# The end of a diagonal-prefix-sum kernel reshaped: diagonal of the last rows first, last 128 rows folded on TensorE, last groups in halves

## The chip, the cores and the metric

The kernel runs on one core of a Trainium2 chip. The metric is device time in microseconds (us); a quoted time is the median of the runs of one kernel. The profile is one execution, and its span is some 2 us shorter than the time of the same run. Engines are named as in the profile: PE is TensorE, DVE is VectorE, ACT is ScalarE, POOL is GpSimd, SP is SyncE.

## The reference

```python
B, H, W = 4, 4224, 4224                      # x: (B, H, W) float32
ps   = np.cumsum(np.cumsum(x, axis=1), axis=2)
diag = np.diagonal(ps, axis1=1, axis2=2)     # (B, 4224)
return np.cumsum(diag, axis=1).astype(np.float32)
```

The element (i, i) of a 2-D prefix sum is the sum of the square up to row i and column i. Going from i-1 to i adds one row part (row i, columns up to i) and one column part (column i, rows above i). So each of the four matrices needs all its 71 MB once, and one number for each diagonal position comes out.

## The kernel before

A group is 384 rows, three to a partition; a matrix has 11 groups. One load brings a group into a strip and turns it into bf16 on the way. ACT and DVE sum the row parts. PE sums the columns with a selector of ones. For the square block on the diagonal, DVE multiplies with a triangular mask. The strip pool has six buffers. The loads are issued from POOL, in the order in which POOL's instructions stand. A scheduler in the build decides that order for the first three matrices.

```python
head = last.tile([P, HEAD], FP32, name="head")            # last 128 rows, last 1056 columns
nc.sync.dma_start(out=head, in_=x[LB, TB:N, N - HEAD : N])

def load_group(b, g):                                     # issued from POOL
    t = strips.tile([P, F, N], BF16, name="strip")
    ...
    nc.gpsimd.dma_start(out=t, in_=x[b, r0:r0+GW, :].rearrange("(p f) w -> p f w", f=F))
    return t

prefetched = {(0, g): load_group(0, g) for g in range(2)}
# ... masks and constants, among them
            um = consts.tile([P, P * f], BF16, name=f"um_{f}_{q}")
            nc.vector.memset(um, 1.0)
            nc.gpsimd.affine_select(out=um, in_=um, ..., pattern=[[1, P * f]], ...)
# ...
    nc.gpsimd.iota(apart_i, ...)                          # POOL
    nc.vector.tensor_copy(out=apart, in_=apart_i)         # DVE: int to float, "the cast"
    nc.gpsimd.affine_select(out=apart, in_=apart, ...)    # POOL: "the mask"; the load behind it waits too
```

The last matrix (b = 3) ends with 256 rows, two to a partition, and then 128 rows, one to a partition. Before, both are summed by ACT and DVE piece by piece as the loads land, and the final row of 128 results is built on one partition and stored:

```python
fin = psum_s.tile([1, P], FP32, name="fin")
matmul(fin, htot, wtri, start=True)
# for each loaded piece of the last 128 rows:
    nc.vector.reduce_sum(out=tsum[:, k:k+1], in_=tail[:, 0, c0:c1], axis=AX.X)
    matmul(fin, tsum[:, k:k+1], wtri)
yl = last.tile([1, P], FP32, name="yl")
nc.vector.tensor_add(out=yl, in0=fin, in1=lc[:, 1, gw:GW])
nc.sync.dma_start(out=out[b, TB:N].unsqueeze(0), in_=yl)
```

Of the kernel before, what the change touches and what calls it, by code (L numbers as in the profile page):

```python
# [8 lines left out]
FP32 = mybir.dt.float32  # L9
# [8 lines left out]
def kernel(  # L18
# [12 lines left out]
    N = H  # L31
# [20 lines left out]
    HEAD = 1056  # L52
    TB = N - P
    head = last.tile([P, HEAD], FP32, name="head")
    nc.sync.dma_start(out=head, in_=x[LB, TB:N, N - HEAD : N])

    def load_group(b, g):
        t = strips.tile([P, F, N], BF16, name="strip")
        r0 = g * GW
        nc.gpsimd.dma_start(  # L60
            out=t,
            in_=x[b, r0 : r0 + GW, :].rearrange("(p f) w -> p f w", f=F),
        )
        return t
# [12 lines left out]
    def upper_masks(f):  # L77
        ums = []
        for q in range(f):
            um = consts.tile([P, P * f], BF16, name=f"um_{f}_{q}")  # L80
# [7 lines left out]
                pattern=[[1, P * f]],  # L88
# [5 lines left out]
    um3 = upper_masks(F)  # L94
# [44 lines left out]
    um2 = upper_masks(2)  # L139
    um1 = upper_masks(1)[0]  # L140
# [13 lines left out]

    def matmul(o, lhsT, rhs, start=False):
        nc.tensor.matmul(  # L156
            o, lhsT=lhsT, rhs=rhs, start=start, stop=False, skip_group_check=True
        )

    DUMP = 2176  # L160

# [7 lines left out]
    def scalar_cols(g):  # L169
# [4 lines left out]
    hsum = last.tile([P, 2], FP32, name="hsum")  # L174
    hmu = last.tile([P, P], BF16, name="hmu")
    nc.vector.reduce_sum(out=hsum[:, 0:1], in_=head, axis=AX.X)
    nc.vector.scalar_tensor_tensor(
        out=hmu,
        in0=head[:, HEAD - P : HEAD],
        scalar=1.0,  # L180
        in1=um1,
        op0=ALU.mult,
        op1=ALU.mult,
        accum_out=hsum[:, 1:2],
    )
    htot = last.tile([P, 1], FP32, name="htot")
    nc.vector.tensor_sub(out=htot, in0=hsum[:, 0:1], in1=hsum[:, 1:2])
# [19 lines left out]
    for b in range(B):  # L207
        whole = b < LB
        ng = NG if whole else NG - 1
        d = psum_d.tile([NG, GW], FP32, name="d")  # L210
        d_last = None
        if not whole:
            d_last = psum_s.tile([1, GW], FP32, name="d_last")

        rs = smalls.tile([P, NG, F], FP32, name="rs")
        ru = smalls.tile([P, NG, F], FP32, name="ru")
        sa = smalls.tile([P, NG, F], FP32, name="sa")
        rows = smalls.tile([P, NG, F], FP32, name="rows")
        nc.vector.memset(sa[:, 0, :], 0.0)  # L219

        first = {"d": True, "l": True}

        def columns(j, lo, hi, rhs):

            if j < ng:
                matmul(d[:, lo:hi], selector(j), rhs, start=first["d"])
                first["d"] = False
            else:
                matmul(d_last[:, lo:hi], ones_col, rhs, start=first["l"])
                first["l"] = False  # L230

        for g in range(ng):
            lo, hi = g * GW, (g + 1) * GW
            strip = prefetched.pop((b, g), None)
            if strip is None:
                strip = load_group(b, g)
            ws = scalar_cols(g)
            for q in range(F):
                mu = mup.tile([P, GW], BF16, name="mu")
                nc.vector.scalar_tensor_tensor(  # L240
                    out=mu,
                    in0=strip[:, q, lo:hi],
                    scalar=1.0,
                    in1=um3[q],
                    op0=ALU.mult,
                    op1=ALU.mult,
                    accum_out=ru[:, g, q : q + 1],
                )
# [36 lines left out]
        if whole:  # L285
            continue
# [113 lines left out]
```

## Time and profile before

| | before |
|---|---|
| time, first three runs | 675.43 us (674.44 to 675.74) |
| span of the profiled run | 672.8 us |
| DVE, PE busy | 39%, 35% of the span |
| written by the loads | 217 GB/s in nearly every slice |
| last load lands (its issue plus "us to landing") | 634.5 + 28.8 = 663.3 us |
| last store issued, and the span's end after it | 670.82 us, 1.98 us |

The page of the kernel before. The rows DMA and GB/s have one figure for each of 40 equal slices of the span; a 9 is 90% or more.

```profile
span 672.8 us, 2608 instructions
...
DMA  9999999999999999999999999999999999999994
GB/s 202 217 215 218 217 217 217 217 217 217 217 219 217 217 218 217 217 217 217 217 217 218 218 217 217 217 215 217 218 217 217 217 217 218 217 217 217 217 201 76
```

The load queue never runs dry until the last slice. So the time is the bytes, plus what comes before the first byte and after the last one.

The start in the timeline of POOL (start, duration, line and instruction, and in brackets what ended the idle time):

```profile
1.32 1.19 POOL L60 DMA_DIRECT2D strip<-in_x_dram  x2 [0.80 <-POOLq L384]
...
6.01 0.58 POOL L60 DMA_DIRECT2D strip<-in_x_dram  x1
38.57 0.19 POOL L130 TENSOR_SCALAR_AFFINE_SELECT apart<-apart 11x11 f32<-11x11 f32 x1 [31.98 <-DVE apart L129]
...
39.49 1.61 POOL L60 DMA_DIRECT2D strip<-in_x_dram  x3
```

Two strips are asked for at 1.32 us, a third at 6.01 (strips are counted from 0, so the third load brings strip 2). Then POOL stands for 32 us in front of the mask of `apart`, which waits for DVE's cast. Nobody is hurt, because the third load is already in the queue.

The last load of the kernel before, in the timeline of POOL and then in its DMA issues (KB, us from issue to landing):

```profile
634.53 0.53 POOL L308 DMA_DIRECT2D strip<-in_x_dram  x1 [14.41 <-DMA strip<-in_x_dram]
```

```profile
strip<-in_x_dram POOLq DMA_DIRECT2D x1, 132.0 KB, 28.8
```

The end in the timeline, the last DVE steps and the last store (SPq):

```profile
665.40 0.96 DVE L362 TENSOR_REDUCE tsum<-strip 128x1 f32<-128x792 bf16 x1
...
666.36 1.23 DVE L362 TENSOR_REDUCE tsum<-strip 128x1 f32<-128x1056 bf16 x1
...
667.89 1.00 DVE L190 TENSOR_TENSOR_SCAN lc<-ones_row,lcarry,d_last 1x384 f32<-1x384 f32 x1 [0.30 <-PE d_last L156]
668.82 0.67 DVE L362 TENSOR_REDUCE tsum<-strip 128x1 f32<-128x528 bf16 x1
669.42 0.99 DVE L198 TENSOR_TENSOR_SCAN lc<-ones_row,lcarry,lc 1x384 f32<-1x384 f32 x1
...
670.51 0.28 DVE L368 TENSOR_TENSOR yl<-fin,lc 1x128 f32<-1x128 f32 x1
670.82 0.23 SPq L369 DMA_DIRECT2D out_dram<-yl  x1
```

About 7.5 us of serial work (663.3 to 670.8) stand between the last landing and the last store, which itself takes 2.0 us to the end.

### The profile page before, as it was taken

What the parts mean: (1) busy time and instruction counts of PE and PEld (TensorE: products, weight loads), DVE (VectorE), ACT (ScalarE), POOL (GpSimd) and SP (SyncE); (2) the same over time, 40 slices, a digit from 0 to 9 for tenths busy, and PEclk for the clock granted to TensorE, in tenths of its full rate; (3) what the DMA queues carried; (4) which work ended last, traced back from release to release, by engine and by line L of the source; (5) the groups of instructions that cost most, each with busy time, mean ns of one, the idle gap of its engine ahead of it and who ended that gap; (6) DMA issues with size and microseconds to landing.
All of it is one profiled execution on the core that took longest, in us unless ns stands there. A gap on an engine that the chain in (4) does not pass through costs nothing.

```text
span 672.8 us, 2608 instructions
## 1 busy us (share of the span) xinstructions
PE 232.5 (35%) x852; PEld 91.2 (14%) x852; DVE 259.3 (39%) x370; ACT 153.9 (23%) x249; POOL 31.8 (5%) x67
## 2 busy tenths in 40 slices
PE   0073453211155543321116543232204534344213
PEld 0031111000022211100002211110001211111001
DVE  2033333344543223334563222334555222234458
ACT  0011222233301112223420111223440011123342
POOL 3010000000000000000000000000000000100000
PEclk9997766555577766566557766766555776766655
DMA  9999999999999999999999999999999999999994
GB/s 202 217 215 218 217 217 217 217 217 217 217 219 217 217 218 217 217 217 217 217 217 218 218 217 217 217 215 217 218 217 217 217 217 218 217 217 217 217 201 76
DMA packets 7958, 143.23 MB, mean 213 GB/s; under 512 B 861, under 2 KB 1546, under 8 KB 2442
## 3 DMA queue, kind: packets, MB, share of 16 engines
q0 software_dynamic: 7712, 142.47, 99.0%
q1 hardware_dynamic: 234, 0.61, 0.3%
q8 instruction: 6, 0.10, 0.1%
q14 instruction: 6, 0.05, 0.0%
HBM read 285.47 MB, written 0.07 MB: 424 GB/s over the span
## 4 chain that ended last, share of the span: by engine, by line
another core or an unknown queue 51%; DVE 36%; DMA 11%; issue 1%; POOL 0%; PE 0%; DVEq 0%; POOLq 0%
DVE rs L252 24%; DMA strip<-in_x_dram 11%; DVE mu L240 9%; DVE lrs L334 1%; DVE c L198 1%; DVE c L190 1%; DVE y L281 0%; DVE y L273 0%; DVE tsum L362 0%; POOL strip L60 0%; DVE lc L190 0%; DVE lc L198 0%; PE d_last L156 0%; DVEq L240 0%
## 5 line engine op out<-in xcount | busy, mean ns | idle before, releaser
L165 ACT ACTIVATE dump<-strip 128x192 bf16<-128x192 bf16 (+11 forms) x124 | 141.1, 1138 | 507.7 <-DMA strip<-in_x_dram 505.1
L240 DVE SCALAR_TENSOR_TENSOR mu<-strip,um 128x384 bf16<-128x384 bf16 x129 | 65.5, 554 | 380.9 <-DMA strip<-in_x_dram 380.9
L252 DVE TENSOR_REDUCE rs<-strip 128x3 f32<-128x1152 bf16 (+10 forms) x43 | 169.8, 3950 | 27.5 <-DMA strip<-in_x_dram 27.5
L156 PE MATMUL d<-mu,sel 128*11 128x384 bf16 x129 | 59.2, 476 | 318.8 <-DVE mu L240 318.5
L156 PE MATMUL d<-strip,sel 128*11 128x384 bf16 x630 | 161.9, 431 | 0.0
L156 PEld LDWEIGHTS <-sel 128*11 128x11 bf16 (+1 forms) x794 | 86.7, 109 | 538.8 <-issue 515.2
L60 POOL DMA_DIRECT2D strip<-in_x_dram x43 | 23.0, 535 | 507.5 <-PE d L156 256.7
L156 PE MATMUL d_last<-strip,sel 128*1 128x384 bf16 (+1 forms) x32 | 14.2, 477 | 84.8 <-DMA strip<-in_x_dram 84.8
L165 ACT ACTIVATION_READ_ACCUMULATOR dump<-strip 128x1 f32 x124 | 23.1, 186 | 0.0
L156 PE MATMUL d<-ident,rows 128*11 128x128 f32 (+1 forms) x24 | 5.8, 415 | 19.9 <-DVE sa L219 13.2
L240 DVE DVE_READ_ACCUMULATOR mu<-strip,um 128x1 f32 x129 | 10.5, 82 | 0.0
L156 PEld LDWEIGHTS d<-ident,rows 128*11 128x11 f32 (+1 forms) x24 | 2.7, 128 | 24.0 <-DVE sa L219 15.0
L156 PE MATMUL fin<-wtri,tsum 128*1 128x128 f32 x8 | 2.4, 401 | 6.7 <-DVE tsum L362 3.9
L334 DVE TENSOR_REDUCE lrs<-strip 128x2 f32<-128x1664 bf16 (+2 forms) x3 | 4.4, 1459 | 0.0
L198 DVE TENSOR_TENSOR_SCAN c<-ones_row,c 11x384 f32<-11x384 f32 (+1 forms) x4 | 3.8, 940 | 0.0
L190 DVE TENSOR_TENSOR_SCAN c<-ones_row,d 11x384 f32<-11x384 f32 (+1 forms) x4 | 3.7, 935 | 0.0
L308 POOL DMA_DIRECT2D strip<-in_x_dram x3 | 1.6, 538 | 43.1 <-DMA strip<-in_x_dram 28.5
L362 DVE TENSOR_REDUCE tsum<-strip 128x1 f32<-128x792 bf16 (+2 forms) x3 | 2.9, 952 | 0.0
L156 PE MATMUL d_last<-mu,sel 128*1 128x256 bf16 x2 | 0.8, 396 | 5.5 <-DVE mu L316 5.5
L304 POOL DMA_DIRECT2D strip<-in_x_dram x3 | 2.1, 708 | 6.7 <-DMA strip<-in_x_dram 6.7
L82 POOL TENSOR_SCALAR_AFFINE_SELECT um<-um 128x384 bf16<-128x384 bf16 (+2 forms) x6 | 2.4, 434 | 0.1
L281 DVE TENSOR_TENSOR y<-y,c 11x384 f32<-11x384 f32 (+1 forms) x4 | 2.2, 545 | 0.1
(56 smaller groups left out, 24.1 us busy)
## 6 DMA issues: line engine op xcount, KB each, us to landing
strip<-in_x_dram POOLq DMA_DIRECT2D x43, 3168.0 KB, 81.7
strip<-in_x_dram POOLq DMA_DIRECT2D x1, 832.0 KB, 72.7
strip<-in_x_dram POOLq DMA_DIRECT2D x1, 672.0 KB, 75.2
head<-in_x_dram SPq DMA_DIRECT2D x1, 528.0 KB, 3.8
strip<-in_x_dram POOLq DMA_DIRECT2D x1, 416.0 KB, 69.8
strip<-in_x_dram POOLq DMA_DIRECT2D x1, 396.0 KB, 56.5
strip<-in_x_dram POOLq DMA_DIRECT2D x1, 264.0 KB, 43.1
strip<-in_x_dram POOLq DMA_DIRECT2D x1, 192.0 KB, 69.4
```

What stands on the lines that cost most here:

```text
L60: nc.gpsimd.dma_start(out=t, in_=x[b, r0 : r0 + GW, :].rearrange("(p f) w -> p f w", f=F),)
L82: nc.gpsimd.affine_select(out=um, in_=um, compare_op=ALU.is_gt, fill=0.0, base=-q, pattern=[[1, P * f]], channel_multiplier=-f,)
L156: nc.tensor.matmul(o, lhsT=lhsT, rhs=rhs, start=start, stop=False, skip_group_check=True)
L165: nc.scalar.activation(out=dump[:, :w], in_=src, func=ACT.Copy, accum_out=acc)
L190: nc.vector.tensor_tensor_scan(out=c12[:rows, 0, :width], data0=ones_row[:rows, :width], data1=d, initial=init1, op0=ALU.mult, op1=ALU.add,)
L198: nc.vector.tensor_tensor_scan(out=c12[:rows, 1, :width], data0=ones_row[:rows, :width], data1=c12[:rows, 0, :width], initial=init2, op0=A ...
L240: nc.vector.scalar_tensor_tensor(out=mu, in0=strip[:, q, lo:hi], scalar=1.0, in1=um3[q], op0=ALU.mult, op1=ALU.mult, accum_out=ru[:, g, q ...
L252: nc.vector.reduce_sum(out=rs[:, g, :], in_=strip[:, :, ws:hi], axis=AX.X)
L281: nc.vector.tensor_add(out=y[:ng, :], in0=y[:ng, :], in1=c12[:ng, 1, :])
L304: nc.gpsimd.dma_start(out=strip[:, :2, c0:c1], in_=src[:, :, c0:c1])
L334: nc.vector.reduce_sum(out=lrs[:, :, i + 1], in_=strip[:, :2, c0 + ws : c1], axis=AX.X)
L362: nc.vector.reduce_sum(out=tsum[:, k : k + 1], in_=tail[:, 0, c0:c1], axis=AX.X)
```

## The change

The intent is to shorten those 7.5 us. The diagonal blocks of the last 384 rows are loaded at the very start, so that these rows end as plain row sums. The last 128 rows are weighted and summed on PE, which folds their 3968 columns into 256, and DVE sums these. The last two full groups are loaded in halves, so that about half of their row sums is done before the group is complete. In each group PE's column matmuls stand ahead of the diagonal products. The last matrix is built in program order and not by the scheduler. Cut to its core:

```diff
-    head = last.tile([P, HEAD], FP32, name="head")
-    nc.sync.dma_start(out=head, in_=x[LB, TB:N, N - HEAD : N])
+    head_a = last.tile([P, 2, GW], FP32, name="head_a")
+    nc.sync.dma_start(out=head_a, in_=x[LB, T0:TB, T0:N].rearrange("(p f) w -> p f w", f=2))
+    head_b = last.tile([P, HB], FP32, name="head_b")
+    nc.sync.dma_start(out=head_b, in_=x[LB, TB:N, N - HB : N])
...
-    def load_group(b, g):
+    def load_group(b, g, cut=0):
+        if cut:
+            nc.gpsimd.dma_start(out=t[:, :, :cut], in_=src[:, :, :cut])
+            nc.gpsimd.dma_start(out=t[:, :, cut:], in_=src[:, :, cut:])
...
-            um = consts.tile([P, P * f], BF16, name=f"um_{f}_{q}")
+            um = consts.tile([P, w], BF16, name=f"um_{f}_{q}")
...
-                pattern=[[1, P * f]],
+                pattern=[[1, w]],
...
-    um2 = upper_masks(2)
+    um2 = upper_masks(2, GW)                 # 256 columns become 384
...
+        if not whole:
+            ctx.enter_context(tc.manual_schedule())
...
-        tcuts = [N - HEAD, 1584, 528, 0]
+        tcuts = [(2176, N - HB), (640, 2176), (128, 640), (0, 128)]
...
-        fin = psum_s.tile([1, P], FP32, name="fin")       # sums by DVE, row on one partition
-        ...
-        nc.sync.dma_start(out=out[b, TB:N].unsqueeze(0), in_=yl)
+        fold = psum_s.tile([P, 2 * P], FP32, name="fold")
+        matmul(fold[:, 0:1], wtri, hrow[:, 2:3], start=True)
+        for c0, c1 in tcuts:
+            if c0 == 0:
+                matmul(fold[:, 0:1], lc[:, 1, 2 * P : GW], ones_row[:1, :1])
+            while c0 < c1:
+                w = min(2 * P, c1 - c0)
+                matmul(fold[:, :w], wtri_h, tail[:, 0, c0 : c0 + w])
+                c0 += w
+        yl = last.tile([P, 1], FP32, name="yl")
+        nc.vector.reduce_sum(out=yl, in_=fold, axis=AX.X)
+        nc.sync.dma_start(out=out[b, TB:N].unsqueeze(1), in_=yl)   # one number from each partition
```

What the build makes of POOL's order, before and after (cut from the listings of the built programs, not a profile). Only the place of one load changes:

```
before: ... iota apart_i, 3 selects of um, iota wtri_i, LOAD strip 2, mask apart, mask wtri, LOAD strips 3, 4, 5
after:  ... iota apart_i, 3 selects of um, iota wtri_i, mask apart, LOAD strip 2, mask wtri, LOAD strips 3, 4, 5
```

More of the change, by code (lines that the diff above doesn't have):

```diff
@@ L49 @@
     )
-    HEAD = 1056
     TB = N - P
-    head = last.tile([P, HEAD], FP32, name="head")
-    nc.sync.dma_start(out=head, in_=x[LB, TB:N, N - HEAD : N])
-    def load_group(b, g):
+    T0 = N - GW
+    HB = 2 * P
+    head_a = last.tile([P, 2, GW], FP32, name="head_a")
+    nc.sync.dma_start(
+        out=head_a, in_=x[LB, T0:TB, T0:N].rearrange("(p f) w -> p f w", f=2)
+    )
+    head_b = last.tile([P, HB], FP32, name="head_b")
+    nc.sync.dma_start(out=head_b, in_=x[LB, TB:N, N - HB : N])
+    def load_group(b, g, cut=0):
         t = strips.tile([P, F, N], BF16, name="strip")
         r0 = g * GW
-        nc.gpsimd.dma_start(
-            out=t,
-            in_=x[b, r0 : r0 + GW, :].rearrange("(p f) w -> p f w", f=F),
-        )
+        src = x[b, r0 : r0 + GW, :].rearrange("(p f) w -> p f w", f=F)
+        if cut:
+            nc.gpsimd.dma_start(out=t[:, :, :cut], in_=src[:, :, :cut])
+            nc.gpsimd.dma_start(out=t[:, :, cut:], in_=src[:, :, cut:])
+        else:
+            nc.gpsimd.dma_start(out=t, in_=src)
         return t
@@ L75, in selector, with upper_masks @@
         return sel[:, NG - 1 - j : 2 * NG - 1 - j]
-    def upper_masks(f):
+    def upper_masks(f, w):
         ums = []
         for q in range(f):
-            um = consts.tile([P, P * f], BF16, name=f"um_{f}_{q}")
+            um = consts.tile([P, w], BF16, name=f"um_{f}_{q}")
             nc.vector.memset(um, 1.0)
@@ L92, in upper_masks @@
         return ums
-    um3 = upper_masks(F)
+    um3 = upper_masks(F, GW)
     ident = consts.tile([P, P], FP32, name="ident")
@@ L138 @@
     )
-    um2 = upper_masks(2)
-    um1 = upper_masks(1)[0]
+    um2 = upper_masks(2, GW)
+    um1 = upper_masks(1, P)[0]
     wtri_i = consts.tile([P, P], I32, name="wtri_i")
@@ L153 @@
     )
+    wtri_h = consts.tile([P, P], BF16, name="wtri_h")
+    nc.vector.tensor_copy(out=wtri_h, in_=wtri)
     def matmul(o, lhsT, rhs, start=False):
@@ L160 @@
     DUMP = 2176
+    CUT = 2176
     def act_sum(acc, src):
@@ L171, in scalar_cols @@
         return 0 if g == 0 else (g * GW) * 9 // 16 // 32 * 32
-    hsum = last.tile([P, 2], FP32, name="hsum")
-    hmu = last.tile([P, P], BF16, name="hmu")
-    nc.vector.reduce_sum(out=hsum[:, 0:1], in_=head, axis=AX.X)
-    nc.vector.scalar_tensor_tensor(
-        out=hmu,
-        in0=head[:, HEAD - P : HEAD],
-        scalar=1.0,
-        in1=um1,
-        op0=ALU.mult,
-        op1=ALU.mult,
-        accum_out=hsum[:, 1:2],
-    )
-    htot = last.tile([P, 1], FP32, name="htot")
-    nc.vector.tensor_sub(out=htot, in0=hsum[:, 0:1], in1=hsum[:, 1:2])
+    hs = last.tile([P, 3], FP32, name="hs")
+    hu = last.tile([P, 3], FP32, name="hu")
+    hrow = last.tile([P, 3], FP32, name="hrow")
+    hmu_a = last.tile([P, 2, GW], BF16, name="hmu_a")
+    hmu_b = last.tile([P, P], BF16, name="hmu_b")
+    nc.vector.reduce_sum(out=hs[:, 0:2], in_=head_a, axis=AX.X)
+    nc.vector.reduce_sum(out=hs[:, 2:3], in_=head_b, axis=AX.X)
+    for k, o, i, m in (
+        (0, hmu_a[:, 0, :], head_a[:, 0, :], um2[0]),
+        (1, hmu_a[:, 1, :], head_a[:, 1, :], um2[1]),
+        (2, hmu_b, head_b[:, HB - P : HB], um1),
+    ):
+        nc.vector.scalar_tensor_tensor(
+            out=o,
+            in0=i,
+            scalar=1.0,
+            in1=m,
+            op0=ALU.mult,
+            op1=ALU.mult,
+            accum_out=hu[:, k : k + 1],
+        )
+    nc.vector.tensor_sub(out=hrow, in0=hs, in1=hu)
     def scans(d, rows, width, init1, init2, c12):
@@ L205, in scans @@
         )
-    for b in range(B):
-        whole = b < LB
-        ng = NG if whole else NG - 1
-        d = psum_d.tile([NG, GW], FP32, name="d")
-        d_last = None
-        if not whole:
-            d_last = psum_s.tile([1, GW], FP32, name="d_last")
-        rs = smalls.tile([P, NG, F], FP32, name="rs")
-        ru = smalls.tile([P, NG, F], FP32, name="ru")
-        sa = smalls.tile([P, NG, F], FP32, name="sa")
-        rows = smalls.tile([P, NG, F], FP32, name="rows")
-        nc.vector.memset(sa[:, 0, :], 0.0)
-        first = {"d": True, "l": True}
-        def columns(j, lo, hi, rhs):
-            if j < ng:
-                matmul(d[:, lo:hi], selector(j), rhs, start=first["d"])
-                first["d"] = False
-            else:
-                matmul(d_last[:, lo:hi], ones_col, rhs, start=first["l"])
-                first["l"] = False
-        for g in range(ng):
-            lo, hi = g * GW, (g + 1) * GW
-            strip = prefetched.pop((b, g), None)
-            if strip is None:
-                strip = load_group(b, g)
-            ws = scalar_cols(g)
-            for q in range(F):
-                mu = mup.tile([P, GW], BF16, name="mu")
-                nc.vector.scalar_tensor_tensor(
-                    out=mu,
-                    in0=strip[:, q, lo:hi],
-                    scalar=1.0,
-                    in1=um3[q],
-                    op0=ALU.mult,
-                    op1=ALU.mult,
-                    accum_out=ru[:, g, q : q + 1],
-                )
-                columns(g, 0, GW, mu)
-                if ws > 0:
-                    act_sum(sa[:, g, q : q + 1], strip[:, q, :ws])
-            nc.vector.reduce_sum(
-                out=rs[:, g, :], in_=strip[:, :, ws:hi], axis=AX.X
-            )
-            for j in range(g + 1, NG):
-                for q in range(F):
-                    columns(j, 0, GW, strip[:, q, j * GW : (j + 1) * GW])
-        nc.vector.tensor_add(out=rows[:, :ng], in0=rs[:, :ng], in1=sa[:, :ng])
-        nc.vector.tensor_sub(out=rows[:, :ng], in0=rows[:, :ng], in1=ru[:, :ng])
-        for q in range(F):
-            matmul(d[:ng, q : GW : F], rows[:, :ng, q], ident)
-        c12 = smalls.tile([NG, 2, GW], FP32, name="c12")
-        scans(d[:ng, :], ng, GW, 0.0, 0.0, c12)
-        carry_ps = psum_s.tile([NG, 2], FP32, name="carry_ps")
-        matmul(carry_ps[:ng, :], earlier[:ng, :ng], c12[:ng, :, GW - 1], start=True)
-        matmul(carry_ps[:ng, 1:2], apart[:ng, :ng], c12[:ng, 0, GW - 1 : GW])
@@ L270, with between @@
+    def between(b, ng, c12, carry_ps):
         carry = smalls.tile([NG, 2], FP32, name="carry")
@@ L284, with columns @@
         )
+    for b in range(B):
+        whole = b < LB
+        if not whole:
+            ctx.enter_context(tc.manual_schedule())
+        ng = NG if whole else NG - 1
+        d = psum_d.tile([NG, GW], FP32, name="d")
+        d_last = None
+        if not whole:
+            d_last = psum_s.tile([1, GW], FP32, name="d_last")
+        first = {"d": True, "l": True}
+        def columns(j, lo, hi, rhs):
+            if j < ng:
+                matmul(d[:, lo:hi], selector(j), rhs, start=first["d"])
+                first["d"] = False
+            else:
+                matmul(d_last[:, lo:hi], ones_col, rhs, start=first["l"])
+                first["l"] = False
+        rs = smalls.tile([P, NG, F], FP32, name="rs")
+        ru = smalls.tile([P, NG, F], FP32, name="ru")
+        sa = smalls.tile([P, NG, F], FP32, name="sa")
+        rows = smalls.tile([P, NG, F], FP32, name="rows")
+        nc.vector.memset(sa[:, 0, :], 0.0)
+        if not whole:
+            rs2 = last.tile([P, 2, F], FP32, name="rs2")
+            sa2 = last.tile([P, 2, F], FP32, name="sa2")
+            for q in range(2):
+                columns(NG - 1, 0, GW, hmu_a[:, q, :])
+            columns(NG - 1, GW - P, GW, hmu_b)
+            for q in range(2):
+                matmul(d_last[:, q : 2 * P : 2], hrow[:, q : q + 1], ident)
+        for g in range(ng):
+            lo, hi = g * GW, (g + 1) * GW
+            strip = prefetched.pop((b, g), None)
+            cut = 0
+            if strip is None:
+                cut = CUT if not whole and g >= ng - 2 else 0
+                strip = load_group(b, g, cut)
+            ws = scalar_cols(g)
+            if cut:
+                ws1 = cut * 5 // 8 // 32 * 32
+                for q in range(F):
+                    act_sum(sa2[:, g - ng + 2, q : q + 1], strip[:, q, :ws1])
+                nc.vector.reduce_sum(
+                    out=rs2[:, g - ng + 2, :], in_=strip[:, :, ws1:cut], axis=AX.X
+                )
+                ws = cut + (lo - cut) * 5 // 8 // 32 * 32
+            for j in range(g + 1, NG):
+                for q in range(F):
+                    columns(j, 0, GW, strip[:, q, j * GW : (j + 1) * GW])
+            for q in range(F):
+                mu = mup.tile([P, GW], BF16, name="mu")
+                nc.vector.scalar_tensor_tensor(
+                    out=mu,
+                    in0=strip[:, q, lo:hi],
+                    scalar=1.0,
+                    in1=um3[q],
+                    op0=ALU.mult,
+                    op1=ALU.mult,
+                    accum_out=ru[:, g, q : q + 1],
+                )
+                columns(g, 0, GW, mu)
+                if ws > 0:
+                    act_sum(sa[:, g, q : q + 1], strip[:, q, cut:ws])
+            nc.vector.reduce_sum(
+                out=rs[:, g, :], in_=strip[:, :, ws:hi], axis=AX.X
+            )
+        if not whole:
+            nc.vector.tensor_add(out=rs2, in0=rs2, in1=sa2)
+            nc.vector.tensor_add(
+                out=rs[:, ng - 2 : ng], in0=rs[:, ng - 2 : ng], in1=rs2
+            )
+        nc.vector.tensor_add(out=rows[:, :ng], in0=rs[:, :ng], in1=sa[:, :ng])
+        nc.vector.tensor_sub(out=rows[:, :ng], in0=rows[:, :ng], in1=ru[:, :ng])
+        for q in range(F):
+            matmul(d[:ng, q : GW : F], rows[:, :ng, q], ident)
+        c12 = smalls.tile([NG, 2, GW], FP32, name="c12")
+        scans(d[:ng, :], ng, GW, 0.0, 0.0, c12)
+        carry_ps = psum_s.tile([NG, 2], FP32, name="carry_ps")
+        matmul(carry_ps[:ng, :], earlier[:ng, :ng], c12[:ng, :, GW - 1], start=True)
+        matmul(carry_ps[:ng, 1:2], apart[:ng, :ng], c12[:ng, 0, GW - 1 : GW])
@@ L285 @@
         if whole:
+            between(b, ng, c12, carry_ps)
             continue
@@ L293 @@
         nc.vector.tensor_copy(out=lcarry, in_=lcarry_ps)
-        columns(NG - 1, 2 * P, GW, hmu)
-        r0 = ng * GW
-        gw = 2 * P
+        src = x[b, T0:TB, :].rearrange("(p f) w -> p f w", f=2)
         strip = strips.tile([P, F, N], BF16, name="strip")
-        src = x[b, r0 : r0 + gw, :].rearrange("(p f) w -> p f w", f=2)
-        cuts = [r0, 2176, 832, 0]
-        nc.gpsimd.dma_start(out=strip[:, :2, r0:N], in_=src[:, :, r0:N])
-        for c1, c0 in zip(cuts[:-1], cuts[1:]):
+        cuts = [(1920, T0), (640, 1920), (0, 640)]
@@ L304 @@
+        for c0, c1 in cuts:
             nc.gpsimd.dma_start(out=strip[:, :2, c0:c1], in_=src[:, :, c0:c1])
         tail = strips.tile([P, F, N], BF16, name="strip")
-        tcuts = [N - HEAD, 1584, 528, 0]
-        for c1, c0 in zip(tcuts[:-1], tcuts[1:]):
+        tcuts = [(2176, N - HB), (640, 2176), (128, 640), (0, 128)]
+        for c0, c1 in tcuts:
             nc.gpsimd.dma_start(out=tail[:, 0, c0:c1], in_=x[b, TB:N, c0:c1])
-        NP = len(cuts)
-        lrs = last.tile([P, 2, NP], FP32, name="lrs")
@@ L312 @@
-        lru = last.tile([P, 2], FP32, name="lru")
-        lsa = last.tile([P, 2, NP - 1], FP32, name="lsa")
-        for q in range(2):
-            mu = mup.tile([P, GW], BF16, name="mu")
-            nc.vector.scalar_tensor_tensor(
-                out=mu[:, :gw],
-                in0=strip[:, q, r0 : r0 + gw],
-                scalar=1.0,
-                in1=um2[q],
-                op0=ALU.mult,
-                op1=ALU.mult,
-                accum_out=lru[:, q : q + 1],
-            )
-            columns(NG - 1, 0, gw, mu[:, :gw])
-            columns(NG - 1, gw, GW, strip[:, q, r0 + gw : N])
@@ L327 @@
-        nc.vector.reduce_sum(
-            out=lrs[:, :, 0], in_=strip[:, :2, r0 : r0 + gw], axis=AX.X
-        )
-        for i, (c1, c0) in enumerate(zip(cuts[:-1], cuts[1:])):
-            ws = (c1 - c0) // 2
-            for q in range(2):
-                act_sum(lsa[:, q, i : i + 1], strip[:, q, c0 : c0 + ws])
-            nc.vector.reduce_sum(
-                out=lrs[:, :, i + 1], in_=strip[:, :2, c0 + ws : c1], axis=AX.X
-            )
-        l1 = last.tile([P, 2], FP32, name="l1")
-        l2 = last.tile([P, 2], FP32, name="l2")
@@ L339, with to_row @@
-        lrows = last.tile([P, 2], FP32, name="lrows")
-        nc.vector.reduce_sum(out=l2, in_=lsa, axis=AX.X)
-        nc.vector.tensor_sub(out=l2, in0=l2, in1=lru)
-        nc.vector.reduce_sum(out=l1, in_=lrs, axis=AX.X)
-        nc.vector.tensor_add(out=lrows, in0=l1, in1=l2)
-        for q in range(2):
-            matmul(d_last[:, q : gw : 2], lrows[:, q : q + 1], ident)
+        def to_row(a):
+            for q in range(2):
+                matmul(d_last[:, q : 2 * P : 2], a[:, q : q + 1], ident)
@@ L346 @@
+        lsa = last.tile([P, 3, 2], FP32, name="lsa")
+        for i, (c0, c1) in enumerate(cuts):
+            act_sum(lsa[:, i, 0:1], strip[:, 0, c0:c1])
+            if i == 0:
+                act_sum(lsa[:, i, 1:2], strip[:, 1, c0:c1])
+            else:
+                nc.vector.reduce_sum(
+                    out=lsa[:, i, 1:2], in_=strip[:, 1, c0:c1], axis=AX.X
+                )
+            to_row(lsa[:, i, :])
         lc = last.tile([1, 2, GW], FP32, name="lc")
         scans(d_last, 1, GW, lcarry[:, 0:1], lcarry[:, 1:2], lc)
-        nc.sync.dma_start(out=out[b, r0 : r0 + gw].unsqueeze(0), in_=lc[:, 1, :gw])
@@ L351 @@
-        fin = psum_s.tile([1, P], FP32, name="fin")
-        matmul(fin, htot, wtri, start=True)
-        tsum = last.tile([P, 4], FP32, name="tsum")
-        k = 0
-        for i, (c1, c0) in enumerate(zip(tcuts[:-1], tcuts[1:])):
-            if i == 0:
-                ws = (c1 - c0) // 2
-                act_sum(tsum[:, k : k + 1], tail[:, 0, c0 : c0 + ws])
-                matmul(fin, tsum[:, k : k + 1], wtri)
-                k += 1
-                c0 += ws
-            nc.vector.reduce_sum(
-                out=tsum[:, k : k + 1], in_=tail[:, 0, c0:c1], axis=AX.X
-            )
-            matmul(fin, tsum[:, k : k + 1], wtri)
-            k += 1
@@ L367 @@
-        yl = last.tile([1, P], FP32, name="yl")
-        nc.vector.tensor_add(out=yl, in0=fin, in1=lc[:, 1, gw:GW])
-        nc.sync.dma_start(out=out[b, TB:N].unsqueeze(0), in_=yl)
+        between(b, ng, c12, carry_ps)
+        nc.sync.dma_start(out=out[b, T0:TB].unsqueeze(0), in_=lc[:, 1, : 2 * P])
+        fold = psum_s.tile([P, 2 * P], FP32, name="fold")
+        matmul(fold[:, 0:1], wtri, hrow[:, 2:3], start=True)
+        for c0, c1 in tcuts:
+            if c0 == 0:
[4 more added lines that the diff above has]
+                c0 += w
```

## The prediction

> **What bounds it now.** The loads. In the page's 40 slices the DMA share is nine tenths or more in every slice but the last, at 217 GB/s written (424 GB/s read; the Trainium skill, "DMA: Bandwidth & Descriptors", "Where 436 GB/s comes from", gives about 358 per core from HBM, so the trace decides). DVE is busy 39%, PE 35%: shorter compute in the middle buys nothing. Only two places pay: a hole in the load stream, and what follows the last byte. By short windows the stream ends at 662.4 us; the last load lands about 663.4 (issue at 634.5 plus 28.8); the span is 672.8. So 9.4 us follow the last landing: in the timeline DVE scans, carries, three tail sums (0.96, 1.23, 0.67 us), two one-partition scans (1.0 each), an add, then the store (2.0 us from issue to end).
>
> **Intended gain: the tail.** Bytes are equal. My estimate of the new tail from those durations: last group lands 649.8, its shorter reduction (2592 elements at 1.04 ns, against 6.15 us before) ends 654.2, group scans 658.2, the two remaining row reductions 661.4, the one-row scans 664.0, carry and y 665.0. PE folds 3968 columns of the last 128 rows in 17 matmuls; at the granted clock of 0.5 a 384-column one repeats every 0.32 us, so 0.21 to 0.32 us each; the last 128 columns land near 664.2 and the fold ends near 666. One PSUM reduction (0.4 us), then the store of 128 four-byte pieces (2.0 to 2.4 us). End near 669: gain 3.7 us (2.5 to 5), after some 0.8 us lost to smaller packets.
>
> **Cost that the diff does not show: the third strip load.** The instruction order of the built kernels differs on POOL. Before, the third strip load is issued (6.01 us) ahead of the masking of "apart"; after, behind it. That mask waits for DVE's cast of "apart", which stands behind DVE's row sums of strips 0 and 1 and three masked products; in the timeline the cast ran at 38.34 and the mask at 38.57 to 38.76. Strip 1's data ends about 33.7 (landing 34.77). So the queue would hold nothing from about 33.3 (mean over engines) until the load issued at 38.8 delivers, about 1.5 us after issue (first load: issue 1.3, data 2.85), near 40.3. A hole of some 7 us, and since the stream is saturated after it, all of it reaches the end.
>
> **Sum.** 675.4 + 7.0 - 3.7 = 678.7 us; range 675.8 to 681.5. Faster by over 2%: 1%; within 2%: 97%; slower by over 2%: 2%.
>
> **What would show it.** DMA share near zero in windows from about 34 to 40 us; the third strip landing near 56 instead of 49.8; every later group some 7 us later; in the chain of waits the DVE and POOL steps of "apart". After the last landing: 4 to 6 us instead of 9.4, ending in fold on PE, one reduction of yl, one store. The middle keeps 217 GB/s and 15 us per group.
>
> **What would make it wrong.** The third load is not blocked (then about 671.7). The fold at low clock is slower than 0.32 us each, or the scattered four-byte store takes over 3 us: then the tail gains less. The skill's same page ("Specifications") says that pieces under 512 B are read and rewritten; the trace shows 79 ns for a 768-byte packet against 1887 ns for 25 KB, and no smaller load packet. Engine skew of 1 to 2 us at the ends of loads blurs the hole.

## The result

The changed kernel takes 684.3 us (683.34 to 684.54, 4 runs), the kernel before in the same job 674.98 us (4 runs). The ratio is 1.0135 (95% interval 1.0117 to 1.0152). Ratios here are the mean time of one kernel's fast runs over that of the other's of the same rounds, so not quite the ratio of the medians. The change is slower by 1.4%, and 684.3 is above the stated range.

The page of the changed kernel, the same rows:

```profile
span 681.5 us, 2655 instructions
...
DMA  8969999999999999999999999999999999999993
GB/s 199 213 123 223 223 216 214 214 216 215 214 219 220 221 220 214 214 214 218 216 217 221 218 219 214 214 217 219 216 216 221 218 217 214 214 219 208 215 212 73
```

The third slice (34 to 51 us) falls to 123 GB/s. Later slices have the old rate. POOL and DVE at the start of the changed kernel:

```profile
1.31 1.19 POOL L71 DMA_DIRECT2D strip<-in_x_dram  x2 [0.80 <-POOLq L401]
...
38.73 1.06 POOL L138 TENSOR_SCALAR_AFFINE_SELECT apart<-apart 11x11 f32<-11x11 f32 x1 [32.46 <-DVE apart L137]
39.75 0.58 POOL L71 DMA_DIRECT2D strip<-in_x_dram  x1
```

```profile
34.93 1.95 DVE L313 TENSOR_REDUCE rs<-strip 128x3 f32<-128x1728 bf16 x1 [13.08 <-DMA strip<-in_x_dram]
...
38.50 0.15 DVE L137 CAST apart<-apart_i 11x11 f32<-11x11 int32 x1
```

DVE's cast of `apart` (38.50) stands behind the row sum of strip 1, which could only start when that strip landed (34.93), and behind three masked products cut from the view. The mask follows the cast at 38.73, and the third load follows the mask at 39.75. The windows view of the changed kernel shows what the load engines did meanwhile (last two columns: DMA share, GB/s):

```profile
33.00:37.00 4.00, 0.00 (x0) 0.00 (x0) 2.07 (x2) 1.37 (x6) 0.00 (x0) 0.50 0.01 0
37.00:41.00 4.00, 3.59 (x11) 1.32 (x11) 4.00 (x21) 0.00 (x0) 2.26 (x3) 0.50 0.00 0
41.00:45.00 4.00, 4.00 (x25) 2.09 (x24) 0.77 (x5) 0.00 (x0) 2.77 (x5) 0.96 1.11 203
```

The start of strip 2's work on ACT marks its landing. These are one line of the kernel before and one of the changed kernel:

```profile
49.79 0.55 ACT L165 ACTIVATE dump<-strip 128x416 bf16<-128x416 bf16 x1 [13.59 <-DMA strip<-in_x_dram]
```

```profile
57.58 0.55 ACT L177 ACTIVATE dump<-strip 128x416 bf16<-128x416 bf16 x1 [21.23 <-DMA strip<-in_x_dram]
```

So it landed 7.8 us later (57.58 against 49.79). The last load of the changed kernel, in the timeline of POOL and in the DMA issues:

```profile
650.42 0.53 POOL L352 DMA_DIRECT2D strip<-in_x_dram  x1 [7.24 <-DMA strip<-in_x_dram]
```

```profile
strip<-in_x_dram POOLq DMA_DIRECT2D x1, 32.0 KB, 21.2
```

The end of the changed kernel, the last DVE step and the stores (`y` holds the results of the ten full groups, `lc` those of the 256 rows, `yl` the last 128), and the last store's line in the DMA issues:

```profile
672.92 0.28 SPq L240 DMA_DIRECT2D out_dram<-y  x1
...
673.25 0.25 SPq L372 DMA_DIRECT2D out_dram<-lc  x1
...
673.70 0.42 DVE L385 TENSOR_REDUCE yl<-fold 128x1 f32<-128x256 f32 x1 [0.80 <-PE fold L167]
674.15 0.36 SPq L386 DMA_DIRECT2D out_dram<-yl  x1
```

```profile
out_dram<-yl SPq DMA_DIRECT2D x1, 0.5 KB, 6.5
```

The last store is issued at 674.15 and the span ends at 681.5, 7.35 us later. Before it was 1.98 us for the same 512 bytes. The DMA engines are not at work in most of that time, as two lines of the windows view of the changed kernel show (last two columns again DMA share, GB/s):

```profile
675.00:676.00 1.00, 0.00 (x0) 0.00 (x0) 0.00 (x0) 0.00 (x0) 0.00 (x0) 1.00 0.08 1
676.00:677.00 1.00, 0.00 (x0) 0.00 (x0) 0.00 (x0) 0.00 (x0) 0.00 (x0) 0.62 0.00 0
```

The same zero stands in every window after that. So the pieces are on record as moved before 676, but the landing is signalled only at 674.15 + 6.5 = 680.7. What holds the landing back is not in the trace.

All of the difference of the two spans, 681.5 - 672.8 = 8.7 us, can be added up from three places:

| place | before | after | difference |
|---|---|---|---|
| last load lands (issue + landing) | 663.3 | 650.4 + 21.2 = 671.6 | +8.3 |
| from there to the issue of the last store | 7.5 | 2.5 | -5.0 |
| from that issue to the span's end | 1.98 | 7.35 | +5.4 |

Of the first row, 7.8 us are there when strip 2 lands; the other 0.5 us come by the end. Smaller pieces are the likely cause; no run isolates it.

### The profile page after: what moved, and what is told of

It reads as the page before. It is cut to its first block, busy times and chain, and to the rows that moved or that the text cites. A ratio compares the mean times of both kernels' runs of the same rounds, so it can differ in the third digit from the quotient of the medians.

```text
span 681.5 us, 2655 instructions
## 1 busy us (share of the span) xinstructions
PE 230.0 (34%) x872; PEld 97.6 (14%) x872; DVE 254.6 (37%) x367; ACT 156.7 (23%) x255; POOL 35.4 (5%) x69
## 4 chain that ended last, share of the span: by engine, by line
another core or an unknown queue 50%; DVE 34%; DMA 12%; PE 2%; issue 1%; DVEq 0%; POOL 0%; POOLq 0%
DVE rs L313 23%; DMA strip<-in_x_dram 12%; DVE mu L301 9%; PE d L167 1%; DVE rs L292 1%; PE fold L167 1%; DVE c L218 1%; DVE c L210 1%; DVE y L239 0%; PE d_last L167 0%; DVE lsa L364 0%; DVE y L231 0%; DVE rows L322 0%; DVE rows L323 0%
## 5 line engine op out<-in xcount | busy, mean ns | idle before, releaser
L167 PE MATMUL d<-strip,sel 128*11 128x384 bf16 x630 | 177.5, 462 | 353.8 <-DMA strip<-in_x_dram 353.8
L177 ACT ACTIVATE dump<-strip 128x640 bf16<-128x640 bf16 (+12 forms) x127 | 143.6, 1131 | 510.7 <-DMA strip<-in_x_dram 508.1
L313 DVE TENSOR_REDUCE rs<-strip 128x3 f32<-128x2208 bf16 (+11 forms) x43 | 163.5, 3801 | 13.1 <-DMA strip<-in_x_dram 13.1
L167 PEld LDWEIGHTS <-sel 128*11 128x11 bf16 (+1 forms) x792 | 90.0, 114 | 539.0 <-issue 506.6
L167 PE MATMUL d<-mu,sel 128*11 128x384 bf16 x129 | 38.4, 403 | 50.9 <-DVE mu L301 50.9
L167 PE MATMUL d_last<-strip,sel 128*1 128x384 bf16 x30 | 8.7, 410 | 12.1 <-DMA strip<-in_x_dram 12.1
L292 DVE TENSOR_REDUCE rs<-strip 128x3 f32<-128x2496 bf16 x2 | 5.5, 2754 | 5.0 <-DMA strip<-in_x_dram 5.0
L167 PE MATMUL fold<-strip,wtri_h 128*128 128x256 bf16 (+1 forms) x16 | 3.4, 387 | 0.0
L167 PE MATMUL d_last<-ident,lsa 128*1 128x128 f32 x12 | 2.9, 406 | 0.2 <-DVE lsa L364 0.2
```

The costliest lines, as they stand in the source:

```text
L167: nc.tensor.matmul(o, lhsT=lhsT, rhs=rhs, start=start, stop=False, skip_group_check=True)
L177: nc.scalar.activation(out=dump[:, :w], in_=src, func=ACT.Copy, accum_out=acc)
L292: nc.vector.reduce_sum(out=rs2[:, g - ng + 2, :], in_=strip[:, :, ws1:cut], axis=AX.X)
L313: nc.vector.reduce_sum(out=rs[:, g, :], in_=strip[:, :, ws:hi], axis=AX.X)
```

## The experiments

A label that begins with b is the kernel before with an edit; nohalf_row, best and those that begin with a are the changed kernel with edits. The theory after the result had two independent parts. H, the hole: the place of one load in POOL's order costs 7 to 8 us and has nothing to do with the tail. S, the store: 128 pieces of 4 bytes cost over 5 us more than one piece of 512. The rivals were that the later loads are late because of the larger first loads and the halves, that the last store waits behind the two stores just ahead of it, and that the tail gain was never there.

Times below with an interval are from 3 or 5 rounds beside the kernel before. Where "before" is quoted, it is that job's own: 674.39, 674.53 and 674.56 us.

### b_wide: the kernel before with two wider masks

```diff
-            um = consts.tile([P, P * f], BF16, name=f"um_{f}_{q}")
+            um = consts.tile([P, P * 3 if f > 1 else P], BF16, name=f"um_{f}_{q}")
...
-                pattern=[[1, P * f]],
+                pattern=[[1, P * 3 if f > 1 else P]],
...
-                in1=um2[q],
+                in1=um2[q][:, :gw],
```

> The kernel before, with nothing changed but the width of the two masks for the next-to-last 256 rows (256 columns become 384); the build then places the third strip load behind the mask of apart, as in the changed kernel. Theory (the late third load costs its whole hole): third strip lands near 57.4 us instead of 49.8, time near 682.6 us, 7.6 over before. Rival (the 8 us by which the last groups of the changed kernel are late come from the larger first loads and the halves): time within 1 us of before.

Measured: 681.59 us, ratio 1.0107 (1.0093 to 1.0121). POOL of b_wide, and the start of ACT's work on strip 2:

```profile
38.25 0.47 POOL L130 TENSOR_SCALAR_AFFINE_SELECT apart<-apart 11x11 f32<-11x11 f32 x1 [31.99 <-DVE apart L129]
38.68 0.58 POOL L60 DMA_DIRECT2D strip<-in_x_dram  x1
```

```profile
56.84 0.55 ACT L165 ACTIVATE dump<-strip 128x416 bf16<-128x416 bf16 x1 [20.96 <-DMA strip<-in_x_dram]
```

Strip 2 landed at 56.84, 7.05 us late.

Widening two masks from 256 to 384 columns adds a fraction of a microsecond of work and 7.2 us of time. The first loads, the halves and the tail are those of the kernel before, so the rival falls for the hole. A build that only moves the column matmuls ahead of the diagonal products, as the change also does, keeps the old place of the load (built, not run). So it is the masks' width that moves the load, and a_narrow below, which keeps the wide masks but not the wide select, shows that it is the width of the select; why the scheduler weighs it so was not looked into.

### a_pre3: the changed kernel, three strips loaded ahead

```diff
-    prefetched = {(0, g): load_group(0, g) for g in range(2)}
+    prefetched = {(0, g): load_group(0, g) for g in range(3)}
```

> The changed kernel with three strips loaded ahead instead of two, so that the third load is issued near 2 us. Theory: the hole from 33 to 41 us is gone, third strip lands near 50.0, time near 676.6, 7.7 less than the changed kernel; still over before, because of the last store. Rival (hole absorbed elsewhere, the stream itself is slower): gain under 4 us.

Measured: 685.01 us, ratio 1.0154 (1.014 to 1.0168). This missed: nothing was gained. POOL and DVE of a_pre3 show why:

```profile
1.32 1.73 POOL L71 DMA_DIRECT2D strip<-in_x_dram  x3 [0.80 <-POOLq L401]
...
54.26 1.06 POOL L138 TENSOR_SCALAR_AFFINE_SELECT apart<-apart 11x11 f32<-11x11 f32 x1 [47.48 <-DVE apart L137]
55.28 0.58 POOL L71 DMA_DIRECT2D strip<-in_x_dram  x1
```

```profile
49.96 2.46 DVE L313 TENSOR_REDUCE rs<-strip 128x3 f32<-128x2208 bf16 x1 [13.04 <-DMA strip<-in_x_dram]
...
54.03 0.15 DVE L137 CAST apart<-apart_i 11x11 f32<-11x11 int32 x1
```

The third load is early now and lands at 50.03. But the build put the row sums of all strips loaded ahead, now three, in front of the cast. The mask moved to 54.26 and the fourth load behind it to 55.28. The hole is about as long as before, one strip later. The expectation had mended the place of one load and not the wait in front of the next.

### a_row and a_pre3_row: the last row stored as one piece

```diff
-        nc.sync.dma_start(out=out[b, TB:N].unsqueeze(1), in_=yl)
+        yrow_ps = psum_s.tile([1, P], FP32, name="yrow_ps")
+        matmul(yrow_ps, yl, ident, start=True)
+        yrow = last.tile([1, P], FP32, name="yrow")
+        nc.vector.tensor_copy(out=yrow, in_=yrow_ps)
+        nc.sync.dma_start(out=out[b, TB:N].unsqueeze(0), in_=yrow)
```

> The changed kernel, its last result turned into one row on PE (matmul with the identity, copy) and stored as one piece of 512 bytes instead of 128 pieces of 4; the y store still goes 1.2 us before. Theory (the pieces cost): store takes 2.0 us instead of 7.4 from issue to the end, the turn adds about 0.9, time near 679.9. Rival (the last store waits behind the y store just ahead of it): store still takes over 6 us, time near 685.

> Both mends together. Theory: the two costs are independent and add, 684.3 - 7.7 - 4.4 = 672.2, some 0.4% under before; what is left is the intended gain at the end less about 0.6 us of slower loading. Rival (the tail gain was never there): 674.5 or more.

Measured: a_row 678.72 us, ratio 1.0061 (1.0047 to 1.0074); a_pre3_row 679.61 us, ratio 1.0075 (1.0061 to 1.0088). The y store and the last store of a_row, whose span is 676.6 us:

```profile
673.00 0.28 SPq L240 DMA_DIRECT2D out_dram<-y  x1
...
674.62 0.23 SPq L390 DMA_DIRECT2D out_dram<-yrow  x1
```

Turning the column into a row moves the issue from 674.15 to 674.62, 0.5 us where 0.9 were expected, and the end comes 1.98 us after it. The y store still goes 1.6 us ahead, so waiting behind the other stores is not the cause. The time is 1.2 us under the expected 679.9. a_pre3_row missed its time for the reason of a_pre3: it still has the hole, one strip later.

### a_narrow and a_narrow_row: the hole mended by the select's width

The 128 new mask columns are all ones anyway, so the select can be kept to 256 columns:

```diff
-                out=um,
-                in_=um,
+                out=um[:, : P * f],
+                in_=um[:, : P * f],
...
-                pattern=[[1, w]],
+                pattern=[[1, P * f]],
```

> The changed kernel, its two wide masks cut by the select over their first 256 columns only (the other 128 are all ones anyway, so the values are the same). The build then issues the third load ahead of the mask of apart again. Theory (the issue order of the third load is the cause, and loading three strips ahead failed only because all strips loaded ahead stay in front of the cast of apart on DVE, so that the hole moved behind the third strip): no hole, third strip lands near 50.0, time 676.6 to 677.2. Rival (the hole has another cause): time within 2 us of 684.3.

> The same with the row store. Theory (the two costs add): 678.7 - 7.6 = 671.1, ratio to before 0.995. Rival (the tail gain was never there): 674.5 or more.

Measured: a_narrow 676.31 us, ratio 1.0019 (1.0005 to 1.0032); a_narrow_row 670.81 us, ratio 0.9938 (0.9926 to 0.9951). POOL of a_narrow, and the start of ACT's work on strip 2:

```profile
1.31 1.20 POOL L71 DMA_DIRECT2D strip<-in_x_dram  x2 [0.80 <-POOLq L401]
...
6.00 0.58 POOL L71 DMA_DIRECT2D strip<-in_x_dram  x1
38.77 1.05 POOL L138 TENSOR_SCALAR_AFFINE_SELECT apart<-apart 11x11 f32<-11x11 f32 x1 [32.19 <-DVE apart L137]
```

```profile
50.00 0.55 ACT L177 ACTIVATE dump<-strip 128x416 bf16<-128x416 bf16 x1 [13.62 <-DMA strip<-in_x_dram]
```

The mask still waits for the cast, and still takes 1.05 us. But the load is ahead of it (6.00), and strip 2 lands at 50.00. The same results cost 8 us less. With the row store another 5.5 us go. Together the mends save 13.5 us of 684.3, and the change's own idea then shows: 0.6% faster than before, clear of noise.

### b_col: the kernel before with the column store

```diff
-        nc.sync.dma_start(out=out[b, TB:N].unsqueeze(0), in_=yl)
+        ycol_ps = psum_s.tile([P, 1], FP32, name="ycol_ps")
+        matmul(ycol_ps, yl, ones_row[:1, :1], start=True)
+        ycol = last.tile([P, 1], FP32, name="ycol")
+        nc.vector.tensor_copy(out=ycol, in_=ycol_ps)
+        nc.sync.dma_start(out=out[b, TB:N].unsqueeze(1), in_=ycol)
```

> The kernel before, its last row turned into a column (a one-row matmul and a copy) and stored as 128 pieces of 4 bytes: the store of the changed kernel alone, with the y store long done. Theory (the pieces cost): issue to end 7.4 us instead of 2.0, turn about 0.7, time near 680.5. Rival (it was slow only because it came right behind two other stores): store 2 to 3 us, time near 675.5.

Measured: 682.59 us, ratio 1.0115 (1.0099 to 1.013), 8 us over before; its span is 680.8. The last store of b_col, and the column's line in the DMA issues:

```profile
671.55 0.36 SPq L373 DMA_DIRECT2D out_dram<-ycol  x1
```

```profile
out_dram<-ycol SPq DMA_DIRECT2D x1, 0.5 KB, 8.3
```

Turning the row into a column delays the issue by 0.7 us, and the store takes 9.25 us to the end where 7.4 were expected. The y store was issued 6 us earlier, the lc store 1.2 us earlier. So the store alone carries the price, in either kernel. It was 6.5 us to landing in the changed kernel, 7.1 in a_pre3, 7.2 in a_narrow and 8.3 here; why it varies is not known.

### a_narrow_s4, a_narrow_s16: larger and fewer pieces

A masked matmul spreads the 128 results over 32 partitions of 4 numbers, or 8 of 16:

```diff
-        nc.sync.dma_start(out=out[b, TB:N].unsqueeze(1), in_=yl)
+        S, M = 4, 32                                   # or 16, 8
+        ...                                            # fine[p, n] = (p % S == n); coarse[p, m] = (p // S == m)
+        nc.vector.tensor_scalar(out=ym, in0=fine, scalar1=yl, scalar2=None, op0=ALU.mult)
+        matmul(yp_ps, coarse, ym, start=True)
+        nc.vector.tensor_copy(out=yp, in_=yp_ps)
+        nc.sync.dma_start(out=out[b, TB:N].rearrange("(m n) -> m n", n=S), in_=yp)
```

> The hole mended; the last 128 results stored as 32 pieces of 16 bytes, from 32 partitions, after a masked matmul. So far: 128 pieces of 4 bytes took 6.5 to 8.3 us from issue to landing, one of 512 bytes about 2.0 to the end. Theory A (time goes with the number of pieces): 5.5 us over 128 pieces is 43 ns each, so issue to end about 3.4 us. Theory B (a fixed price as soon as pieces are short): 7 to 9 us as with 4 bytes.

> The same with 8 pieces of 64 bytes. Theory A: issue to end about 2.3 us. Theory B: 7 to 9 us.

Measured (one look each): with 32 pieces of 16 bytes the store landed 1.3 us after its issue and the span ended 2.2 us after it (668.10 to 670.3). With 8 pieces of 64 bytes the end came 2.0 us after the issue (667.40 to 669.4). A fixed price for short pieces (theory B) falls. Theory A expected 3.4 us for 32 pieces, so it does not fit either.

### a_narrow_spread, a_step16, a_step4, a_adj32: the distance of the pieces

These give a wrong result. They store the same four-byte numbers elsewhere in the output, and the right row follows as one piece, as in a_row:

```diff
-        nc.sync.dma_start(out=out[b, TB:N].unsqueeze(1), in_=yl)
+        # a_narrow_spread: 264 bytes apart
+        nc.sync.dma_start(out=out[0:2, :].rearrange("b (p k) -> (b p) k", k=66)[:, 0:1], in_=yl)
+        # a_step16, a_step4: k = 16 or 4, so 64 or 16 bytes apart
+        nc.sync.dma_start(out=out[0, : P * k].rearrange("(p k) -> p k", k=k)[:, 0:1], in_=yl)
+        # a_adj32: only 32 pieces, 4 bytes apart
+        nc.sync.dma_start(out=out[0, :32].unsqueeze(1), in_=yl[:32, :])
```

> Wrong result on purpose: the column of 128 four-byte pieces goes to addresses 264 bytes apart in rows 0 and 1 of the output, and the right last row is stored as one piece after it. Theory A1 (each piece costs, wherever it goes): the column still takes 6.5 us or more to land, the span ends some 7 to 9 us after its issue. Theory A2 (neighbouring pieces that share a short stretch of memory wait for each other): the column lands in 2 to 3 us, and the row store behind it, about 0.7 us later, sets the end, 3 us after the column's issue.

> Wrong result on purpose: 128 four-byte pieces, 64 bytes apart, into row 0; the right row follows as one piece. So far: 4 bytes apart 6.5 to 8.3 us to landing, 264 bytes apart 1.4. Theory 64 (pieces wait for each other only within one 64-byte stretch): 1.4 us. Theory 512 (within one 512-byte stretch, so 8 pieces share one here): clearly over 1.4, at most 3 us.

> Wrong result on purpose: 128 four-byte pieces, 16 bytes apart, so 4 in a 64-byte stretch and 32 in a 512-byte one; the right row follows. Theory 64: about 1.4 to 1.7 us. Theory 512: about a quarter of the extra 5 to 7 us, so 2.5 to 3.5 us. If instead the 128 pieces cost whatever their step below 264 bytes: 6.5 us or more.

> Wrong result on purpose: only 32 four-byte pieces, 4 bytes apart, so 16 in each of two 64-byte stretches and all in one 512-byte stretch; the right row follows. Theory 64 (a stretch of 64 bytes works its 16 pieces off one by one, different stretches side by side): the full 6.5 us or more. Theory 512 (all pieces in 512 bytes one by one): a quarter of the extra, 2.5 to 3.5 us.

Measured (one look each), the column's line in the DMA issues (last figure: us from issue to landing), first of a_narrow_spread, to which those of a_step16 and a_step4 are equal, then of a_adj32:

```profile
out_dram<-yl SPq DMA_DIRECT2D x1, 0.5 KB, 1.4
```

```profile
out_dram<-yl SPq DMA_DIRECT2D x1, 0.1 KB, 3.1
```

| pieces | bytes each | distance | us to landing |
|---|---|---|---|
| 128 | 4 | 4 bytes (touching) | 6.5, 7.1, 7.2, 8.3 |
| 32 | 4 | 4 bytes (touching) | 3.1 |
| 128 | 4 | 16, 64 or 264 bytes | 1.4 |
| 32 | 16 | 16 bytes (touching) | 1.3 |

The number of pieces alone costs nothing visible: 128 of them land in 1.4 us. Being short alone costs nothing visible either. The price appears only where pieces lie 4 bytes apart, and there it grows with their number: (3.1 - 1.4) us over 32 pieces is 53 ns each, (6.5 - 1.4) and (8.3 - 1.4) us over 128 are 40 to 54 ns each. So touching 4-byte pieces look as if their writes were completed one after another. The span agrees: in a_step4 it ends 3.2 us after the column's issue (667.21 to 670.4), with the row store behind it, against 7.35 in the changed kernel. Nor is the touching column cut into more pieces: the SP queue has 648 packets in a_narrow, and 650 in a_step4 with the row besides. Theory 512 fails on a_step4, theory 64 on a_adj32. Which distance between 4 and 16 bytes is the limit, and by what mechanism, was not tried.

### nohalf_row: the last groups loaded whole

```diff
-    CUT = 2176
+    CUT = 0                  # on a_narrow_row; the sums of the first halves are left out too
```

> Both mends, but the last two groups loaded whole, and summed in one piece. Theory (the halves save more after the last load than their smaller packets cost): the last group's reduction is 6.15 instead of 2.85 us and PE's last fold comes 2 to 3 us later, while its last load lands 0.3 us sooner: time near 672.8, ratio to before 0.9972. Rival (halves bought nothing, since the last small loads bound the tail): 670.5 to 671.

Measured: 673.79 us, ratio 0.9983 (0.9968 to 0.9997), against 0.9938 with halves; the time is 1.0 us above the expected 672.8. The last group's reduction in nohalf_row and in a_narrow_row:

```profile
651.36 6.15 DVE L313 TENSOR_REDUCE rs<-strip 128x3 f32<-128x5760 bf16 x1
```

```profile
651.53 2.85 DVE L313 TENSOR_REDUCE rs<-strip 128x3 f32<-128x2592 bf16 x1
```

Both start within 0.2 us of each other. The whole one takes 3.3 us longer, and the last store is issued 3.2 us later (670.30 against 667.14). The halves are worth 3.0 us by the medians, and the rival falls.

### best: a version that beats both

On a_narrow_row, DVE's two late row sums go ahead of its wait for the last group's carry, and PE's first fold matmul goes ahead of the row matmuls:

```diff
-        lcarry = last.tile([1, 2], FP32, name="lcarry")
-        nc.vector.tensor_copy(out=lcarry, in_=lcarry_ps)
+        fold = psum_s.tile([P, 2 * P], FP32, name="fold")
+        matmul(fold[:, 0:1], wtri, hrow[:, 2:3], start=True)
...
+        lcarry = last.tile([1, 2], FP32, name="lcarry")
+        nc.vector.tensor_copy(out=lcarry, in_=lcarry_ps)
         lc = last.tile([1, 2, GW], FP32, name="lc")
         scans(d_last, 1, GW, lcarry[:, 0:1], lcarry[:, 1:2], lc)
...
-        fold = psum_s.tile([P, 2 * P], FP32, name="fold")
-        matmul(fold[:, 0:1], wtri, hrow[:, 2:3], start=True)
```

> The one with both mends, and with DVE's two late row sums moved ahead of the wait for the carry of the last group, and PE's first fold matmul moved ahead of the rows. Theory: PE's folding, which starts some 0.6 us earlier, is what the tail waits for, so 0.5 to 0.9 us less: near 670.4. Rival (the last landing bounds the tail): within 0.2 us of the one without it.

Measured: 670.16 us (669.98 to 670.93), ratio 0.9931 (0.9918 to 0.9945). The last store of best is issued at 666.47 instead of 667.14. The profile agrees with the theory, but the medians differ by 0.65 us and the two intervals overlap, so by time alone this last step is not settled. Against both the kernel before and the changed one it is faster.

## Why the prediction was right or wrong

It was wrong in size: slower was expected, by 3.3 us (678.7 against 675.4), and it came out slower by 9.3 (684.3 against 674.98). The loss at the start came as forecast; the gain of 3.7 us at the end did not come, for after strip 2 the changed kernel loses another 0.9 us (0.5 - 5.0 + 5.4). Point by point:

- **The third strip load: right in mechanism, a little small.** Strip 2 was to land near 56 and landed at 57.58, a delay of 7.8 us where 7.0 were put into the sum. One part is the mask: it was taken at its old 0.19 us and took 1.06. It ran beside DVE's masked products (38.58 to 39.73). The Trainium skill ("SBUF — State Buffer", "SBUF: two separate sides") says that a DVE instruction with two inputs from SBUF and a GpSimd instruction that reads SBUF lock each other out of one shared port pair: the one that starts first holds it to its end. The traces fit that, though no run isolates it: the mask ends at 39.79, just after the second product (39.73), and in b_wide at 38.72, just after a product that ends at 38.64. One term was right by luck: 1.5 us from issue to data was read off the first load ("data 2.85"), but by the packets in that trace only `head` moves until 3.48; after the hole the first packet came at 41.0, 1.3 us after the issue. b_wide and a_narrow show the hole itself.
- **Smaller packets: about right.** 0.8 us were put down; 0.5 us came between strip 2 and the last landing.
- **The work between the last landing and the last store: right.** Landing near 664.2 and issue near 666.5 (the fold's 666 and a 0.4 us sum) make 2.3 us; the trace has 2.5. The 15 back-to-back fold matmuls took 3.13 us, 0.21 us each; the granted clock was 0.50 in the windows from 670 to 672 us and 0.59 in the one after. The Trainium skill ("TensorE: Matmul & The Clock Gate", "Wait — 56ns, not 53.3ns?") states N / 1.2 GHz from start to start in a cold array, which makes an estimate of 0.213 us for 256 columns, and the trace agrees.
- **The failed step: "then the store of 128 four-byte pieces (2.0 to 2.4 us)".** It took 7.35 us from issue to the end. The term of the sum was mis-sized by 5.0 us (7.35 against 2.4). From the last landing to the end the prediction had 4.8 us (664.2 to 669); it took 9.9 (671.6 to 681.5), and the store is 5.0 of these 5.1 us. In spans the whole miss is 8.7 - 3.3 = 5.4 us; the hole, 0.8 us longer, and the smaller packets, 0.3 us cheaper, make up about the rest. The risk was named ("takes over 3 us"), but the range did not include it. The figure started from the last store of the kernel before, a single piece of 512 bytes, so 128 touching pieces were taken to cost hardly more than one. No trace at hand had such a store, so a wide range was due there.
- **Views: half right.** The DMA share was 0.01 and 0.00 from 33 to 41 us, as forecast, and the middle kept its rate. The chain of waits did not name `apart`, as I had said it would: it goes from PE's work on strip 1 (42.19 us) straight into the loads. The hole was found in the timeline of POOL and in the windows.

## What to carry to other kernels

Where loads set the time, compare the built order of the instructions on the engine that issues the loads, not only the diff: a small change of a constant's width moved one load behind a wait and cost 7 us. Issue the loads of the ramp ahead of anything that waits for an engine that waits for those loads; loading one strip more ahead did not help, because the wait grew by one strip too. End with one contiguous piece: turning 128 results from a column into a row cost 0.5 to 0.7 us, and storing the column cost over 5.

## What the Trainium skill lacked or had wrong

- "DMA: Bandwidth & Descriptors" ("Specifications") says that below 512 bytes the engine does read-modify-write. It does not say that the distance of the pieces matters. Here 128 pieces of 4 bytes landed in 1.4 us when they lay 16, 64 or 264 bytes apart and in 6.5 to 8.3 us when they touched; 32 touching pieces of 16 bytes took 1.3 us. Whether read-modify-write is what costs the time was not shown.
- The same page ("Where 436 GB/s comes from") says without a condition that for transfers between HBM and SBUF the HBM side, about 358 GB/s, binds. This kernel, which runs on one core, read 424 GB/s over its whole span. The page's own single-core measurement of 425 GB/s, a section earlier, fits the trace; the sentence lacks that condition.
- No page read says that the scheduler of the build can move a load behind an instruction that waits for other loads, when an unrelated constant changes its width (b_wide: +7.2 us), or that the order should be compared after each change.
